# Six thresholds of a list scheduler and two cuts of a chain: when side work joins TensorE's queue in a hybrid diffusion step

## The chip, the cores and the metric

One core of a Trainium2 chip runs the whole program. The metric is device time in microseconds (us), the median over the runs; lower is better. Engines: TensorE (PE) multiplies, VectorE (DVE), ScalarE (ACT) and GpSimd (POOL) do elementwise work, SyncE (SP) issues the transfers from memory.

## The reference

One inference step of a two-layer backbone over 512 latent and 128 context tokens, width 1024. Cut to what matters:

```python
for l in range(2):
    mod = split(silu(c) @ w_mod[l] + b_mod[l], 6)          # once for latents, once for context
    h = rms_norm(x) * (1 + mod[1]) + mod[0]
    if l == 0:                                             # attention next to Hyena
        p = h @ w_in                                       # q, k, v and three Hyena channels
        q, k = rms_norm(q), rms_norm(k)                    # per head of 128, then rotary
        y = softmax(q k') v ;  z = long_conv(v1 * x1, filters) * x0      # by Fourier transforms
        out = concat(y, z) @ w_out
    else:                                                  # mLSTM, 8 heads, forward and backward scans
        out = (norm(fwd(h) + bwd(h)) * sigmoid(o)) @ w_out
    x = x + mod[2] * rms_norm(out)
    h = rms_norm(x) * (1 + mod[4]) + mod[3]
    x = x + mod[5] * rms_norm((gelu(conv3(h @ wu_g)) * conv3(h @ wu_u)) @ w_down)
```

## The kernel before

All 640 tokens stay on the chip; weights stream through once, in tiles of 128x1024, by SP's queue (tile `wr`). Every large product is computed as three products of a high and a low part, so each weight tile is split first: ACT casts the high part (`wh`), DVE subtracts it from the raw tile to get the low part (`wl`). The activations are split likewise (`a0h`/`a0l` into layer 0's mixer, `a1` into its FFN, `a2` and `a3` in layer 1). `wl155` is the low part of tile 155.

The order of the instructions on each engine is decided while the program is built, by a hand-made list scheduler (class `Order`). A main list of tasks is TensorE's: weight column after weight column. Beside it run side generators: the attention's units, the Hyena's filters and long convolution, the mLSTM's directions, the modulation sections, the norms at the boundaries. Each side yields at its waits. Before each piece of main work `pump` looks at the sides in their order and steps one whose time, `when`, has come on TensorE's planned clock:

```python
if s[3] and not r:
    return max(s[0], self.t["DVE"] - s[3], self.t["ACT"] - s[3])
t = max(s[0], self.t["DVE"] - s[4], self.t["ACT"] - s[4])
```

`s[0]` is when the side's inputs are planned to be ready. `s[3]` is nonzero for the modulation sections alone (SLACK0 to SLACK4): they go on only while DVE and ACT are planned no further than that many ns ahead of TensorE. `s[4]` is the same for all other sides (their lead: HLEAD for Hyena, QLEAD for q, k, v, BLEAD for the boundaries, DLEAD for the mLSTM's directions). If no side can step, `pump` lets the next weight tiles be split (`idle`), until DVE or ACT are planned SPARE ns ahead, or TIGHT ns while a boundary is under way. These numbers do no work; they decide in which order the instructions of the engines stand, and each engine then takes its own in that order.

Products accumulate in PSUM: three buffers of kind `mm` (1024 columns or 640 tokens) and two of kind `aux`, handed on when the reading engine has emptied them; a new product waits for a free one.

What the text speaks of:

- A modulation section (`mod_section`, layer l, section s) multiplies silu(c) into 1024 columns of `w_mod`: DVE multiplies and adds transferred weight tiles `mw` into two accumulators `acc` (latents and context). Sections 2 and 5 then split `acc` (ACT `moda`, DVE `modb`), sum over partitions on TensorE with a matrix of ones (`modp`, four matmuls with `moda`, four with `modb`), and DVE adds the result to the row. `acc12` is layer 1, section 2: the gate behind the mLSTM's output projection.
- `direction`: one head and direction of the mLSTM. TensorE: `mb`, `dl`, `it`, `pi`, `in`, `pc`, small matmuls; DVE between them: the weights `w`, the states `cb` and the sums `nu`, `hs`. `hT` transposes the finished head, `mos` gates it, `o1h`/`o1l` are its parts for the output projection `o`. The projections of the next heads (`mq`, `mk`, `mv`, `mo`) are TensorE's main work around them.
- `forward`/`long_conv`: Hyena. DVE multiplies spectra in a chain of ten instructions per frequency block (`vx`, `vf`, then `vp`, `vm`), before the inverse transform on TensorE (`iy`). `u` are the Hyena's projections, `zh` their convolution, `hyf` the products of its filters.
- `qkv_evac`: for each of five token tiles, q and k are copied (`qsq`), normalised (`qn`), scaled, multiplied with the gain (`qkg`) and rotated (`rope`), and then transposed (`qkt`).
- `fm_first`: the first three weight columns of a projection run side by side over the eight blocks of 128 inputs, the last TAILK blocks column by column.
- `o1` is the boundary behind the mLSTM's output projection: the residual, its norm, transposes (`o1p3nt`), shift and scale (`o1p3ny`), the split (`a3h`, `a3l`), then the up-projection (`g10l`, `u10l`: the last 256 tokens of its first columns).

L284 is the line of the helper that records all operations of DVE, ACT, POOL and SP, L365 the matmuls, L376 the transposes: rows are told apart by their tiles.

Of the kernel before, what the change touches and what calls it, by code (L numbers as in the profile page):

```python
# [59 lines left out]
class Order:  # L60
# [7 lines left out]
    LEAD = 3000.0  # L68
    SPARE = 5000.0
    GUARD = 0.0  # L70
    TIGHT = 2000.0
    FIRST = 2500.0

    def __init__(self):
# [116 lines left out]
    def pump(self):  # L191
        while True:
# [7 lines left out]
            else:  # L200
                spare = self.TIGHT if self.urgent else self.SPARE
                if self.urgent:
# [123 lines left out]
def hybrid_step(ctx: ExitStack, tc: tile.TileContext, A: dict, O: dict):  # L326
# [27 lines left out]
    def mm(name):  # L354
        t = mmp.tile([P, 1024], F32, tag="mm", name=name)
        od.got("mm", t)
        return t
# [39 lines left out]
    def rsqrt(ss, n, scale, name, eps=EPS, v=None):  # L397
        y, q, a = (small(name + c, n) for c in "yqa")
        if v is None:
            v = small(name + "v", n)  # L400
            nc.vector.tensor_scalar(v, ss, scale, eps, op0=ALU.mult, op1=ALU.add)
        nc.vector.tensor_scalar(y.bitcast(I32), v.bitcast(I32), -0.5, RSQ, op0=ALU.mult, op1=ALU.add)
        nc.vector.scalar_tensor_tensor(q, v, -0.5, y, op0=ALU.mult, op1=ALU.mult)
        for n in range(3):
            nc.vector.tensor_tensor(a, q, y, op=ALU.mult)
            if n < 2:
                nc.vector.scalar_tensor_tensor(q, a, 1.5, q, op0=ALU.add, op1=ALU.mult)
            nc.vector.scalar_tensor_tensor(y, a, 1.5, y, op0=ALU.add, op1=ALU.mult)
        return y
# [17 lines left out]
                yield  # L427

    EVF = 1
    TAILK = 3  # L430

    def fm_task(src, act, name, evac, needs=()):
        def run(w):
# [89 lines left out]
    def fm_first(specs, act):  # L523
# [9 lines left out]
        def all_(_):  # L533
            ps = []
            for n in range(3):
                od.take("mm")
                ps.append(mm(specs[n][1]))
            seq = [(k, n) for k in range(KT - TAILK) for n in range(3)]
            seq += [(k, n) for n in range(3) for k in range(KT - TAILK, KT)]
            for k, n in seq:  # L540
# [368 lines left out]
    HYE = nc.vector  # L909
    ROPE = nc.gpsimd  # L910
    SLACK1 = 1500.0
    SLACK2 = 2000.0
    SLACK3 = 500.0
    SLACK4 = 500.0

    def spawn_mods(slack, *sections, keys=()):
        def run(_):
            od.spawn(mod_chain(sections, keys), low=slack, rank=MRANK)
            yield
        return Task(run)  # L920
# [105 lines left out]
    def boundary(pss, tiles, l, s, xs, nxt, name, key, pages=None):  # L1026

        n = len(tiles)
        ss = small(name + "ss", n)
        t = {}  # L1030
        yield [("mod", l, s)] + [("mod", 1, 4)] * (l == 0 and s == 5)
        junk = page(name + "j").bitcast(BF)[:, 0:D]
        if WARM and tiles[0] == 0 and nxt is not None:
            nc.scalar.activation(ones1, ones[:, 0:1], AF.Gelu if s == 2 else AF.Exp)
        for j, i in enumerate(tiles):
            if nxt is not None and i >= ROWS:
                t[i] = mw.tile([P, D], F32, tag="mw", name=f"{name}t{i}")
            else:
                t[i] = row(f"{name}t{i}")
            nc.scalar.activation(junk, pss[i], AF.Square, accum_out=ss[:, j : j + 1])  # L1040
            nc.vector.tensor_tensor(t[i], pss[i], mods[l, s, 0 if i < 4 else 1], op=ALU.mult)
            od.gave("mm", pss[i])
            yield 0
        od.side_after(ss)
        yield
        r = rsqrt(ss, n, 1.0 / D, name)
        for j, i in enumerate(tiles):
            nc.vector.scalar_tensor_tensor(xs[i], t[i], r[:, j : j + 1], xs[i], op0=ALU.mult, op1=ALU.add)
            yield 0
            if nxt is None:  # L1050
                nc.sync.dma_start(O["y"][i * P : (i + 1) * P, :], xs[i])
        if nxt is None:
            return
        yield from pre_norm(xs, tiles, l + (s == 5), 3 if s == 2 else 0, nxt, name + "n", key, t, pages)
# [57 lines left out]
    def forward(src, cols, out, name):  # L1112
# [24 lines left out]
        for n, (o, x, y, op) in enumerate(((out[0][:, a], c[:, a], c[:, b], ALU.add), (out[0][:, b], c[:, a], c[:, b], ALU.subtract),  # L1137
# [5 lines left out]
            nc.vector.tensor_tensor(o, x, y, op=op)  # L1143
            if FINE and n % FINE == FINE - 1:
                yield 0
        yield

    FINE = 0

    def filters():  # L1150
        z, w = hy["z"], hy["w"]
# [160 lines left out]
    def long_conv(hf):  # L1312
# [17 lines left out]
        HYE.tensor_tensor(vp[:, h1], vp[:, h1], gr, op=ALU.mult)  # L1330
        if FINE:
            yield 0
# [8 lines left out]
        for n in range(2):  # L1341
# [4 lines left out]
            HYE.tensor_tensor(S, S, gc, op=ALU.mult)  # L1346
            if FINE:
                yield 0
            nc.vector.tensor_tensor(x[0], x[0], x[1], op=ALU.subtract)
            nc.vector.tensor_tensor(C, C, S, op=ALU.add)  # L1350
            if FINE:
                yield 0
# [41 lines left out]

    QROWS = 2
    QACT = 1
    QSCALE = 1

    def qkv_evac(ps, i):
        yield [("qk", j) for j in range(i - QROWS)]  # L1400
# [18 lines left out]
        r = rsqrt(ss, 6, 1.0 / DH, f"qn{i}")  # L1419
        if QSCALE:  # L1420
            for a in range(6):
# [116 lines left out]
    def out_proj(mix, wname, order, l, nxt, xs, halves, name):  # L1538
# [9 lines left out]
        for t in tm_tasks(  # L1548
                lambda k, i, g: [x[:, i * P : (i + 1) * P] for x in cur[k]],
                lambda k: A[wname][order[k] * P : (order[k] + 1) * P, :], KT, halves, name,  # L1550
                lambda ps, t: od.spawn(boundary(ps, t, l, 2, xs, nxt, f"{name}p{t[0]}", "af", name),
                                       lead=BLEAD, urgent=True),
                prep=prep, needs=lambda k, g: [key(q) for q in range(KT)], stay=STAY[l], whole=True,
# [39 lines left out]
    def ffn(l, act, nxt, xs):  # L1593
        hid, cur = {}, {}
        specs = up_specs(l, act, hid)
        ka, kb = (("af", l, h[0]) for h in HALVES)
        ts = fm_head(specs[:NPRE], act, ka, kb)
        ts += [fm_task(s, act, n, f) for s, n, f in specs[NPRE:]]

        def prep(k, g):  # L1600
            c0, c1 = HALVES[g][0] * P, HALVES[g][-1] * P + P
            hh, hl = page(f"hh{l}{k}{g}", FR), page(f"hl{l}{k}{g}", FR)
            split(hh[:, 0 : c1 - c0], hl[:, 0 : c1 - c0], hid[k][:, c0:c1])
            cur[g, k] = hh, hl

        for t in tm_tasks(
                lambda k, i, g: [x[:, (i - HALVES[g][0]) * P : (i - HALVES[g][0]) * P + P] for x in cur[g, k]],
                lambda k: A["w_down"][l, k * P : (k + 1) * P, :], NJ, HALVES, f"dn{l}",
                lambda ps, t: od.spawn(
                    finish_last(ps, t, l, xs) if l == 1 and t == HALVES[1]  # L1610
                    else boundary(ps, t, l, 5, xs, nxt, f"f{l}p{t[0]}", "am"), lead=FLEAD, urgent=True),
                prep=prep, tail=l == 1):
            ts += t
        return ts
# [251 lines left out]
    def head_mix(h):  # L1866
# [30 lines left out]
        for d in range(2):  # L1897
            od.spawn(direction(h, d, q, v1, kw[d], ssb, cb[d], hs, co), lead=DLEAD)
        yield [("hs", h)]
# [56 lines left out]
    J1 = 1  # L1956
    QLEAD = 6000.0
    ALEAD = 6000.0
    BLEAD = 4000.0
    FLEAD = 1000.0  # L1960
    MLEAD = 2500.0
    TLEAD = 1500.0
    DLEAD = 1750.0
    OLEAD = 5000.0
    ms = [x for i in range(4) for x in (4 + i, 8 + i)]
    k0, k1 = act_keys("am", 0, HALVES[0]), act_keys("am", 0, HALVES[1])
# [35 lines left out]
    act2 = Lazy("a2")  # L2002
    tasks.append(spawn_mods(SLACK2, (1, 0), (1, 1), (0, 5), (1, 3), (1, 4), keys=[("hid", 0, J0)]))
    tasks += ffn(0, act1, act2, xs)
# [299 lines left out]
```

## Time and profile before

| what | value |
|---|---|
| median of 3 runs | 1741.65 us (1736.06 to 1744.64) |
| the profiled execution's own time | 1739.15 us |
| its span in the profile | 1737.3 us |
| PE busy | 1683.4 us, 97% of the span |
| DVE, ACT, POOL busy | 1243.6, 746.3, 353.8 us |
| transfers | 203.85 MB, 117 GB/s on average |

A matmul shows as busy from its start to its modelled end, and neighbours overlap, so the busy time tells where TensorE stood still and not how fast it went. How fast is told by the granted clock (PEclk): 1.00 is 2.4 GHz, 0.50 is 1.2 GHz, and a stretch of 20 us at 0.66 is one in which some of the time was at the lower of the two.

### The profile page before, as it was taken

The numbers are of one execution on the slowest core, as the hardware profiler recorded it, in microseconds if no ns is written. First come the engines' busy times: TensorE is split into PE (matmuls) and PEld (weight loads), VectorE is DVE, ScalarE is ACT, GpSimd is POOL, SyncE is SP. The second block draws the span as 40 slices with busy tenths as digits, with TensorE's granted clock in tenths as the row PEclk, the third lists the DMA queues.
The fourth block names the chain that finished last, engine by engine and source line by source line (L and its number), as shares of the span: only waits on it lengthen the run. The fifth ranks groups of instructions, "written<-read, shape, count | busy, mean of one in ns | idle before, by whom it ended". The sixth has DMA issues, their size and how long they took to land. (4 is left out here: it accounts for less than half of the span.)

```text
span 1737.3 us, 25489 instructions
## 1 busy us (share of the span) xinstructions
PE 1683.4 (97%) x10074; PEld 1523.0 (88%) x10074; DVE 1243.6 (72%) x2057; ACT 746.3 (43%) x1233; POOL 353.8 (20%) x187
## 2 busy tenths in 40 slices
PE   7899899999999999999999999997999999999997
PEld 2778787789999999888899999996899999998886
DVE  4788797878878888797766888886578744445365
ACT  3422545545434344455565344334354423333343
POOL 0000121001546454340013111120015411111000
PEclk9999999999999999999999999998999999999999
DMA  9245132412434434454523212122124322223343
GB/s 359 91 152 170 37 101 101 169 38 99 158 121 143 144 119 154 153 198 129 188 89 137 70 47 83 57 69 100 49 77 147 125 77 74 73 74 109 132 159 122
DMA packets 64352, 203.85 MB, mean 117 GB/s; under 512 B 7335, under 2 KB 12455, under 8 KB 64234
## 3 DMA queue, kind: packets, MB, share of 16 engines
q1 hardware_dynamic: 64234, 202.23, 33.9%
q8 instruction: 79, 1.29, 0.3%
q14 instruction: 39, 0.32, 0.1%
HBM read 196.17 MB, written 3.94 MB: 115 GB/s over the span
## 5 line engine op out<-in xcount | busy, mean ns | idle before, releaser
L284 DVE TENSOR_TENSOR wl<-wr,wh 128x1024 fp32r<-128x1024 f32 (+1 forms) x260 | 317.9, 1228 | 107.8 <-ACT wh L284 107.6
L284 ACT CAST wh<-wr 128x1024 fp32r<-128x1024 f32 (+1 forms) x260 | 263.5, 1018 | 146.7 <-PE dn L365 104.1
L284 POOL TENSOR_TENSOR hid<-zg,zu 128x640 f32<-128x640 f32 x44 | 105.5, 2398 | 318.5 <-DVE zu L284 305.9
L284 DVE SCALAR_TENSOR_TENSOR acc<-mw,sc,acc 128x1024 f32<-128x1024 f32 x91 | 168.3, 1868 | 2.7 <-DMA mw<-in_w_mod 2.4
L284 POOL TENSOR_TENSOR acc<-acc,modp 128x1024 f32<-128x1024 f32 x49 | 146.2, 2984 | 115.4 <-ACT modp L284 91.2
L284 DVE SCALAR_TENSOR_TENSOR zg<-g,vec,zg 128x127 f32<-128x127 f32 (+3 forms) x168 | 87.4, 541 | 89.4 <-ACT zg L284 86.4
L365 PE MATMUL dn<-wh,hh 128*128 128x512 f32 x440 | 139.1, 396 | 1.8 <-DVE zu L284 1.6
L365 PE MATMUL dn<-wl,hh 128*128 128x512 f32 x440 | 138.2, 394 | 0.0
L365 PE MATMUL dn<-wh,hl 128*128 128x512 f32 x440 | 138.1, 394 | 0.0
L284 DVE SCALAR_TENSOR_TENSOR zu<-u,vec,zu 128x511 f32<-128x511 f32 (+2 forms) x164 | 86.7, 549 | 62.8 <-ACT zu L284 59.9
L284 ACT ACTIVATE zu<-u,vec 128x640 f32<-128x640 f32 (+1 forms) x42 | 36.8, 876 | 173.8 <-PE u L365 173.8
L365 PE MATMUL u<-a3h,wh 128*128 128x384 f32 (+1 forms) x336 | 104.7, 312 | 0.8 <-DVE a3h L284 0.8
L365 PE MATMUL g<-a3h,wh 128*128 128x384 f32 (+1 forms) x336 | 104.8, 312 | 0.0
L365 PE MATMUL g<-a1h,wh 128*128 128x384 f32 (+1 forms) x336 | 104.8, 312 | 0.0
L365 PE MATMUL u<-a3l,wh 128*128 128x384 f32 (+1 forms) x336 | 104.1, 310 | 0.5 <-POOL a3l L284 0.5
L365 PE MATMUL u<-a3h,wl 128*128 128x384 f32 (+1 forms) x336 | 104.3, 310 | 0.2 <-DVE wl L284 0.2
L365 PE MATMUL u<-a1h,wl 128*128 128x384 f32 (+1 forms) x336 | 104.2, 310 | 0.2 <-DVE wl L284 0.2
L365 PE MATMUL u<-a1h,wh 128*128 128x384 f32 (+1 forms) x336 | 104.2, 310 | 0.0
L365 PE MATMUL g<-a3h,wl 128*128 128x384 f32 (+1 forms) x336 | 104.1, 310 | 0.0
L365 PE MATMUL g<-a3l,wh 128*128 128x384 f32 (+1 forms) x336 | 104.1, 310 | 0.0
L365 PE MATMUL g<-a1h,wl 128*128 128x384 f32 (+1 forms) x336 | 104.0, 310 | 0.0
L365 PE MATMUL u<-a1l,wh 128*128 128x384 f32 (+1 forms) x336 | 104.0, 310 | 0.0
(742 smaller groups left out, 4452.2 us busy)
## 6 DMA issues: line engine op xcount, KB each, us to landing
wr<-in_w_up SPq DMA_DIRECT2D x92, 512.0 KB, 3.3
wr<-in_w_down SPq DMA_DIRECT2D x82, 512.0 KB, 3.3
mw<-in_w_mod SPq DMA_DIRECT2D x80, 512.0 KB, 4.4
wr<-in_w_ml SPq DMA_DIRECT2D x34, 512.0 KB, 3.6
wr<-in_w_out SPq DMA_DIRECT2D x18, 512.0 KB, 4.2
wr<-in_w_in SPq DMA_DIRECT2D x13, 512.0 KB
wr<-in_w_u SPq DMA_DIRECT2D x12, 512.0 KB, 5.2
we<-in_w_mod SPq DMA_DIRECT2D x8, 512.0 KB, 7.3
```

Source lines behind the costliest of these rows:

```text
L284: r = f(*args, **kw)
L365: r = nc.tensor.matmul(out, lhsT, rhs, start=start, stop=stop)
```

## The change

The weights, the transfers and the products stay the same; TensorE's generated order has 8181 rows in both. Six numbers move thresholds or leads of the scheduler. FINE lets the Hyena's DVE chain yield after every second product, so that other instructions can be put between. QSCALE moves the scaling of q and k from ACT (six multiplies of 128x128 per token tile) to DVE (one multiply of 128x768 with the factor broadcast), five token tiles in all.

```diff
--- before.py
+++ after.py
@@ -68,7 +68,7 @@
     LEAD = 3000.0
     SPARE = 5000.0
     GUARD = 0.0
-    TIGHT = 2000.0
+    TIGHT = 6000.0
     FIRST = 2500.0
 
     def __init__(self):
@@ -427,7 +427,7 @@
                 yield
 
     EVF = 1
-    TAILK = 3
+    TAILK = 2
 
     def fm_task(src, act, name, evac, needs=()):
         def run(w):
@@ -909,7 +909,7 @@
     HYE = nc.vector
     ROPE = nc.gpsimd
     SLACK1 = 1500.0
-    SLACK2 = 2000.0
+    SLACK2 = 4000.0
     SLACK3 = 500.0
     SLACK4 = 500.0
 
@@ -1145,7 +1145,7 @@
                 yield 0
         yield
 
-    FINE = 0
+    FINE = 2
 
     def filters():
         z, w = hy["z"], hy["w"]
@@ -1394,7 +1394,7 @@
 
     QROWS = 2
     QACT = 1
-    QSCALE = 1
+    QSCALE = 0
 
     def qkv_evac(ps, i):
         yield [("qk", j) for j in range(i - QROWS)]
@@ -1956,11 +1956,11 @@
     J1 = 1
     QLEAD = 6000.0
     ALEAD = 6000.0
-    BLEAD = 4000.0
+    BLEAD = 6000.0
     FLEAD = 1000.0
     MLEAD = 2500.0
     TLEAD = 1500.0
-    DLEAD = 1750.0
+    DLEAD = 4000.0
     OLEAD = 5000.0
     ms = [x for i in range(4) for x in (4 + i, 8 + i)]
     k0, k1 = act_keys("am", 0, HALVES[0]), act_keys("am", 0, HALVES[1])
```

The generated order, at three places.

TensorE at the start of the mLSTM's output projection, where head 7's last main work `mo7` ends and the first tiles `o10_0`, `o10_1` begin. Before:

```order
L365 MATMUL mo7_11153<-a2l7_7690,wh154_10884 128x256
L365 MATMUL in71_11233<-v17_9003,w71_10986 128x129 x4
L365 MATMUL pc71_11254<-kw71_10839,v17_9003 128x128
L365 MATMUL pc71_11254<-v17_9003,kw71_10839 128x1
L365 MATMUL modp1200_11282<-moda120_11262,onesr_91 128x512
L365 MATMUL modp1200_11282<-modb120_11263,onesr_91 128x512
L376 MATMUL hT7_11286<-ident_86,hs7_10917 128x128 x5
L365 MATMUL modp1201_11303<-moda120_11262,onesr_91 128x512
L365 MATMUL modp1201_11303<-modb120_11263,onesr_91 128x512
L365 MATMUL o10_0_11311<-wh155_11016,o1h0_11020 128x512 x2
L365 MATMUL o10_0_11311<-wh155_11016,o1l0_11021 128x512 x2
```

The same place now:

```order
L365 MATMUL mo7_11197<-a2l7_7665,wh154_10952 128x256
L376 MATMUL hT7_11277<-ident_86,hs7_10899 128x128 x5
L365 MATMUL o10_0_11284<-wh155_11076,o1h0_11080 128x512 x2
L365 MATMUL o10_0_11284<-wh155_11076,o1l0_11081 128x512 x2
L365 MATMUL o10_0_11284<-wl155_11077,o1h0_11080 128x512 x2
L365 MATMUL o10_1_11301<-wh155_11076,o1h0_11080 128x512 x2
L365 MATMUL o10_1_11301<-wh155_11076,o1l0_11081 128x512 x2
L365 MATMUL o10_1_11301<-wl155_11077,o1h0_11080 128x512 x2
```

The last scan's `in71` and `pc71` and the partition sums `modp` of section (1,2) are gone from here (the sums stand among `mk5` and `mo2`, the scan among `mo5` and `mo6`); the transposes `hT7` follow `mo7`, and the projection follows them.

DVE when head 4's two directions begin. Before:

```order
L284 TENSOR_TENSOR kw40_9932<-kT4_9926,col_8329 128x640
L284 TENSOR_TENSOR kw41_9934<-kT4_9926,col_8329 128x640
L284 SCALAR_TENSOR_TENSOR acc120_8352<-mw126_8992,sc_93,acc120_8352 128x1024
L284 SCALAR_TENSOR_TENSOR w40_9966<-mb40_9963,col_8329,msk_7719 128x128 x5
L284 SCALAR_TENSOR_TENSOR zmq5_9986<-mq5_9897,vec_84,zmq5_9986 128x511 x2
L284 SCALAR_TENSOR_TENSOR zmq5_9986<-mq5_9897,vec_84,zmq5_9986 128x127 x2
L284 TENSOR_TENSOR wl146_9993<-wr146_9683,wh146_9992 128x1024
L284 SCALAR_TENSOR_TENSOR cb40_9922<-cb40_9922,wsb_8387,dl40_10023 128x129 x3
L284 SCALAR_TENSOR_TENSOR zmq5_9986<-tmq5_10030,zmq5_9986 128x640
L284 SCALAR_TENSOR_TENSOR w41_10048<-mb41_10045,col_8329,msk_7719 128x128 x5
L284 SCALAR_TENSOR_TENSOR zmk5_10068<-mk5_9998,vec_84,zmk5_10068 128x511 x2
```

The same place now:

```order
L284 TENSOR_TENSOR kw40_9903<-kT4_9897,col_8304 128x640
L284 TENSOR_TENSOR kw41_9905<-kT4_9897,col_8304 128x640
L284 TENSOR_TENSOR modb120_9932<-acc120_8327,moda120_9931 128x1024
L284 SCALAR_TENSOR_TENSOR w40_9938<-mb40_9935,col_8304,msk_7694 128x128 x5
L284 SCALAR_TENSOR_TENSOR cb40_9893<-cb40_9893,wsb_8362,dl40_9946 128x129 x3
L284 SCALAR_TENSOR_TENSOR w41_9956<-mb41_9953,col_8304,msk_7694 128x128 x5
L284 SCALAR_TENSOR_TENSOR cb41_9894<-cb41_9894,wsb_8362,dl41_9976 128x129 x3
L284 SCALAR_TENSOR_TENSOR zmq5_9995<-mq5_9880,vec_84,zmq5_9995 128x511 x2
L284 SCALAR_TENSOR_TENSOR zmq5_9995<-mq5_9880,vec_84,zmq5_9995 128x127 x2
L284 TENSOR_TENSOR wl146_10002<-wr146_9673,wh146_10001 128x1024
L284 TENSOR_TENSOR nu40_10020<-it40_10021,col_8304 128x516
L284 TENSOR_TENSOR acc120_8327<-modp1200_10036,modn12_9929 128x512
```

The second direction (`w41`, `cb41`) comes right behind the first, ahead of the next head's convolution `zmq5` and the split `wl146`, and the modulation section's `modb120` and its first sum stand here; `modb120` stood some 150 rows later before.

DVE in layer 0, in the second half of q, k, v and Hyena, where the split `wl24` for the last Hyena projections stands. Before:

```order
L284 TENSOR_TENSOR vf13_1598<-vf13_1598,g1c_953 128x512
L284 TENSOR_TENSOR vx01_1873<-vx01_1873,vx11_1874 128x512
L284 TENSOR_TENSOR vf12_1597<-vf12_1597,vf13_1598 128x512
L284 TENSOR_TENSOR vp11_1971<-vx01_1873 128x256
L284 TENSOR_TENSOR vp11_1971<-vf12_1597 128x256
L284 TENSOR_TENSOR vm11_1972<-vx01_1873 128x256
L284 TENSOR_TENSOR vm11_1972<-vf12_1597 128x256
L284 SCALAR_TENSOR_TENSOR zh1_2001<-u1_1919,vec_84,zh1_2001 128x511 x2
L284 SCALAR_TENSOR_TENSOR zh1_2001<-u1_1919,vec_84,zh1_2001 128x127 x2
L284 TENSOR_TENSOR wl24_2015<-wr24_1757,wh24_2014 128x1024
L284 TENSOR_TENSOR qsq3_1779<-qsq3_1779,rope_1119 128x6x64 x2
```

The same place now:

```order
L284 TENSOR_TENSOR qsq4_1799<-qsq4_1799,qn4y_1922 128x768
L284 TENSOR_TENSOR qsq3_1780<-qsq3_1780,qkg_1121 128x768
L284 TENSOR_TENSOR vx01_1758<-vf12_1611,g1c_953 128x512
L284 TENSOR_TENSOR vx11_1759<-vf13_1612,g1s_972 128x512
L284 TENSOR_TENSOR vf12_1611<-vf12_1611,g1s_972 128x512
L284 TENSOR_TENSOR vf13_1612<-vf13_1612,g1c_953 128x512
L284 SCALAR_TENSOR_TENSOR zh1_1989<-u1_1914,vec_84,zh1_1989 128x511 x2
L284 SCALAR_TENSOR_TENSOR zh1_1989<-u1_1914,vec_84,zh1_1989 128x127 x2
L284 TENSOR_TENSOR wl24_2003<-wr24_1741,wh24_2002 128x1024
L284 TENSOR_TENSOR qsq3_1780<-qsq3_1780,rope_1119 128x6x64 x2
L284 SCALAR_TENSOR_TENSOR zh2_2052<-u2_1995,vec_84,zh2_2052 128x511 x2
L284 SCALAR_TENSOR_TENSOR zh2_2052<-u2_1995,vec_84,zh2_2052 128x127 x2
```

Six instructions of the chain (the two sums, `vp11`, `vm11`) went behind `wl24`; the scaling of `qsq4` on DVE, and ahead of it its eleven small instructions `qn4`, went in front.

## Rows read from the trace of the kernel before

**Rows 1.** Page: busy share in 40 slices of the span, and granted clock.

```profile
PE   7899899999999999999999999997999999999997
...
PEclk9999999999999999999999999998999999999999
```

**Rows 2.** Waits of TensorE: for what, us in total, times, longest.

```profile
PE modp L365 <- ACT moda L284: 6.3, 1, 6.3
PE qkv L365 <- DVE wl L284: 4.4, 1, 4.4
PE u L365 <- DVE wl L284: 3.5, 3, 3.1
```

**Rows 3.** Windows: length, busy by engine (instructions), PEclk, DMA share, GB/s.

```profile
180.00:200.00 20.00, 15.56 (x80) 12.98 (x79) 13.56 (x41) 8.82 (x35) 1.96 (x2) 0.91 0.19 53
240.00:260.00 20.00, 16.85 (x104) 16.59 (x103) 19.56 (x36) 4.60 (x13) 7.39 (x4) 0.91 0.08 27
...
405.00:880.00 475.00, 473.58 (x2869) 441.99 (x2869) 378.09 (x461) 223.81 (x288) 178.43 (x70) 1.00 0.43 147
947.00:1180.00 233.00, 232.45 (x1718) 230.82 (x1717) 193.06 (x472) 96.88 (x199) 40.75 (x29) 1.00 0.21 68
1180.00:1200.00 20.00, 11.28 (x54) 9.16 (x53) 16.45 (x37) 8.64 (x20) 1.49 (x1) 0.66 0.44 155
1260.00:1300.00 40.00, 37.57 (x253) 35.98 (x253) 30.97 (x75) 22.82 (x40) 6.36 (x6) 1.00 0.23 75
```

**Rows 4.** Timeline of TensorE, start of the output projection.

```profile
1190.01 0.79 PE L365 MATMUL modp<-moda,onesr 128*128 128x512 f32 x1 [6.25 <-ACT moda L284]
1191.27 0.79 PE L365 MATMUL modp<-modb,onesr 128*128 128x512 f32 x1 [0.47 <-DVE modb L284]
1194.06 1.30 PE L376 MATMUL hT<-ident,hs 128*128 128x128 f32 x5 [2.00 <-DVE hs L284]
...
1198.57 1.05 PE L365 MATMUL o<-wh,o1h 128*128 128x512 f32 x2
...
1199.95 0.63 PE L365 MATMUL o<-wl,o1h 128*128 128x512 f32 x2
1200.42 0.39 PE L365 MATMUL modp<-moda,onesr 128*128 128x512 f32 x1
```

**Rows 5.** Timeline of DVE, layer 0, second half.

```profile
230.88 2.36 DVE L284 TENSOR_TENSOR wl<-wr,wh 128x1024 fp32r<-128x1024 f32 x2 [1.14 <-ACT wh L284]
...
242.90 2.06 DVE L284 TENSOR_TENSOR vx<-vf,g1c 128x512 f32<-128x512 f32 x1
...
248.33 0.68 DVE L284 TENSOR_TENSOR vx<-vx,vx 128x512 f32<-128x512 f32 x1
...
250.87 2.16 DVE L284 SCALAR_TENSOR_TENSOR zh<-u,vec,zh 128x511 f32<-128x511 f32 x4
252.95 1.22 DVE L284 TENSOR_TENSOR wl<-wr,wh 128x1024 fp32r<-128x1024 f32 x1
...
258.46 0.16 DVE L284 TENSOR_SCALAR qn4v<-qss 128x6 f32<-128x6 f32 x1
...
260.21 0.17 DVE L284 SCALAR_TENSOR_TENSOR qn4y<-qn4a,qn4y 128x6 f32<-128x6 f32 x1
```

**Rows 6.** Timeline of POOL, same place.

```profile
242.25 2.16 POOL L284 TENSOR_TENSOR vx<-zh,vx 128x640 f32<-128x640 f32 x1 [19.29 <-ACT qj L284]
```

**Rows 7.** Timeline of TensorE, same place.

```profile
254.22 0.69 PE L365 MATMUL u<-a0h,wl 128*128 128x384 f32 x1 [3.15 <-DVE wl L284]
```

**Rows 8.** Tile qsq: operation, count, ns min/median/max, first and last start.

```profile
L284 ACT ACTIVATE qsq<-qsq,qn4y x6: 384/386/403, 260.4 to 261.9; 128x128 f32<-128x128 f32 x6
...
L284 DVE TENSOR_TENSOR qsq<-qsq,qkg x5: 948/949/953, 194.7 to 263.6; 128x768 f32<-128x768 f32 x5
```

**Rows 9.** Timeline of all engines, mLSTM, head 1.

```profile
984.72 1.12 DVE L284 SCALAR_TENSOR_TENSOR cb<-cb,wsb,dl 128x129 f32<-128x129 f32 x3 [0.40 <-PE dl L365]
...
986.27 1.06 PE L365 MATMUL it<-cb,zmq 128*128 128x129 f32 x8
```

## The prediction

> **What bounds the kernel now.** I read the page first: TensorE is busy in nearly every slice, and the dips are few and sharp [rows 1]. So time can be won only where TensorE stands still or runs at the lower clock, and lost only where a new wait appears. The table of its waits says which ones end last: one of 6.3 us for a modulation section's cast, 4.4 us for a weight split in the first half of layer 0, 3.1 us of the 3.5 for the split in its second half [rows 2]. The windows say how much the rest can give: the FFN of layer 0 has 473.58 us of 475 busy, the mLSTM 232.45 of 233, both at clock 1.00; the start of the output projection has only 11.28 of 20, at 0.66 [rows 3]. Transfers and the total of DVE's work end no such wait, so I go by places and not by engine totals. All sums are against the profiled execution (1739.15 us); the median lies 2.5 us above it.
>
> **Start of the output projection.** Before, TensorE reaches the section's sums with nothing else to do: 6.25 us for `moda`, 0.47 for `modb`, 2.00 for `hs`, together 8.72 us [rows 4]. The wait comes from the order: the cast stands behind the last head's work on ACT and DVE, and the transposes of the last head and all of the projection stand behind the sums on TensorE. Behind the idle time the clock fell: the window's 0.66 of 20 us says 6.8 us lost, so 13.6 us at 1.2 GHz [rows 3]. The `modp` at 1190.01 lasts 0.79 us and that at 1200.42 0.39, and the pairs of `o` fall from 1.05 to 0.63 between 1198.57 and 1199.95 [rows 4], so the low stretch is 1186.0 to 1199.6. In it TensorE idled 4.0 + 0.47 + 2.00 us and worked 7.1, of which half, 3.55, is lost. The place costs 8.72 + 3.55 = 12.3 us.
>
> In the new order the sums stand a whole head earlier, the last scan's `in71` and `pc71` too, so `hs7` is long done when `mo7` ends; `hT7` and then `o10_0` follow without a wait. The eight `modp` are moved and cost the same at full clock. What may come instead: the third token tile needs the PSUM buffer that `hT7` leaves, which `mos7` on DVE frees, and `mos7` now stands behind four tiles' splits. I put 0.3 us there, with bounds of 0 and 2.0 (the size of the wait for `hs` that it replaces). **-12.0 us** (-12.3 to -10.3).
>
> **What that puts into the mLSTM.** DVE takes over two `modb`, each a 128x1024 subtract like `wl` at 1.22 us, and four sums of 128x512 at some 0.68 like `vx` [rows 5]: 5.2 us. DVE works 193.06 of 233 us there [rows 3], so 40 us are free and the work fits; the cover is gone only where a direction is due. DLEAD lets DVE take up a direction while it is further ahead in its plan, and puts both directions back to back. In the trace of before, `cb` of head 1 ended at 985.84 and `it` began at 986.27: a margin of 0.43 us and no wait [rows 9]. After the change most of the 16 directions should run at such margins. A small matmul that waits holds up all main work behind it on TensorE. If every second direction waits for a tenth of a us it is 0.8; if all wait 0.25, 4.0. I take the nearest row, which is no wait at 0.43 of margin, and add a little: **+0.5** (0 to +4).
>
> **Layer 0, second half.** The split `wl24` came 3.15 us late [rows 7], and the window's 0.91 of 20 us means 3.6 us at 1.2 GHz [rows 3], nearly all of it busy behind the wait: 1.7 lost. FINE takes six instructions of the chain away from in front of it, 248.33 to 250.87, 2.5 us [rows 5]. But the order also puts two scalings in front, which cost 0.95 each by the gain multiply of the same shape [rows 8], and the eleven instructions `qn4`, 258.46 to 260.38 or 1.9 us [rows 5]: 3.8 us. Against that, the six products of the first chain move ahead of `wl22`, where DVE waited 1.14 us for ACT [rows 5]; and the multiplies beside POOL's work took 2.06 us instead of 0.68 at worst [rows 5, 6], which may fall otherwise. So the wait becomes 3.15 - 2.5 + 3.8 - 1.14 = 3.3 if the multiplies are as slow as before, and about 0.5 if they are not (some 2.8 us less over the four). I take 1.5, and that the clock then stays up (if not, 1.7 come back): -1.65 - 1.7 = -3.3. The transposes of the last tiles and the inverse transform now come before scores that waited little before; I give 1.3 us back. ACT is spared 5 x 6 multiplies of 0.386 us and reading gaps [rows 8], but nothing waits for ACT for long there. **-2** (-4 to +2).
>
> A rule speaks against this part. The multiply `vx` that began at 242.90 beside POOL's operation of 2.16 us ended with it [rows 5, 6]. The Trainium skill, "SBUF — State Buffer", section "Who interferes with whom", says that a VectorE instruction with two SBUF inputs and a GpSimd instruction that reads SBUF exclude each other for a whole instruction; this trace agrees at 242.90. QSCALE's new multiplies are of that kind, while ACT's were not; by the rule the sum would be that of the second rival.
>
> **First half of layer 0.** The 4.4 us for a split [rows 2] and the 0.91 behind it [rows 3] stay: there DVE's rows are in the same order as before, FINE's yields notwithstanding. **0.**
>
> **Boundary o1.** 40 us lose 2.4 [rows 3], all in waits for the last normalised blocks. TIGHT and BLEAD put three weight splits ahead of the norm's small chain, where DVE idled, and the transposes of the last two token tiles about nine matmuls earlier; TAILK moves the last blocks' use. I take **-1.5** (-2.4 to +1).
>
> **FFN of layer 0.** SLACK2 lets the modulation's multiply-adds go ahead of some splits; 97 us of DVE are free in 475 [rows 3], TensorE loses 1.4 in all, so nothing to win. **0** (0 to +2). The filters' products in layer 0 change places with projections: **-0.5** (-2 to +1.5). FFN of layer 1 and the end have the same order.
>
> Sum: -12.0 + 0.5 - 2 + 0 - 1.5 + 0 - 0.5 = -15.5, so 1723.65 against 1739.15, and 1741.65 - 15.5 = 1726 for the median.
>
> **Rivals.**
> 1. *The directions eat half.* Speaking for it: margins of 0.43 us where there were often several, and DVE with 5 us more. Against: no wait in the two heads that already ran this way. At 0.4 us over 16 directions, 6.4 instead of 0.5: 1732.
> 2. *POOL and the scalings collide.* The two scalings ahead of `wl24` each last as long as POOL's operation, 2.16 instead of 0.95, and push two products into the same: up to 4 us more in front of `wl24`, so the wait is 5.5 and the low clock (1.7) stays: +5.7, 1732. For it, 242.90; against, POOL's operations there follow the gain multiply, not the scaling.
> 3. *The wait moves and stays.* The projection's next need, `mos7` and the high and low parts of the last heads' outputs, comes so late that TensorE waits over 5 us and the clock falls again: 1726 + 5 + 3.5 = 1735. Against: DVE has 3 us between the end of `mo7` and the third tile for one 0.9 us operation.
> 4. *Slower.* A direction taken up early on DVE holds the splits `wl` and the convolutions of the next head behind it: in-order DVE serves two directions at a stretch, some 8 us with `nu` and `hs`. If a main projection then waits for its `wl` once per head by more than 3 us, as at `wl24`, and the clock falls behind it as there, each head costs 3 + 1.7 = 4.7, eight heads 37.6 against 16 won: 1764. It decides from 3.0 us per head on (24.2 over eight heads takes all of 15.5 and 8.7 beyond). Against: in the mLSTM window TensorE lost 0.55 us in 233 at a DVE load of 83%, so the splits run well ahead.
>
> **Numbers.** The forecast 0.62, rival 1 0.14, rival 2 0.06, rival 3 0.08, slower 0.07, faster than all this (the 4.4 us go too) 0.03. Faster and slower count from 0.5%, 8.7 us, about what a measurement of this kernel can tell from no change: the limit is 1733. The forecast, the last case and half of rivals 1 and 2 lie below it, with some of the forecast's own spread taken off: faster 0.74, same 0.18, slower 0.08. The forecast's bounds are -12.3 - 4 - 2.4 - 2 = -20.7 and -10.3 + 4 + 2 + 1 + 2 + 1.5 = +0.2, hardly all at once; its own range is 1720 to 1732, and the range up to rival 3, 1718 to 1738.
>
> **What would show it.** Right: no wait for `moda` between the mLSTM and the projection, and clock 1.00 in that window; TensorE over 19 us busy there. The mLSTM's window still loses under 2 us. The wait before the last Hyena projections shrinks to 0 to 3 us; that for `qkv` at the first half's end stays at 4.4. The boundary loses about 1 us in 40. Wrong: waits of several tenths at `it`, `pi` or `dl`; a wait of over 2 us at the third token tile; a lower clock anywhere in layer 1.

## The result and the profile after

The changed kernel takes 1727.5 us (median of 5 runs, 1723.8 to 1729.08) against 1740.36 (5 runs, 1736.06 to 1744.64): ratio 0.9924, 95% interval 0.9901 to 0.9947. The profiled execution took 1723.8 us, span 1722.0.

The page of the changed kernel, busy share and granted clock in 40 slices, to lay beside [rows 1]: the dip at three quarters of the line (slice 28) is gone from both.

```profile
PE   7899999999999999999999999999999999999997
...
PEclk9999999999999999999999999999999999999999
```

TensorE's waits after, beside [rows 2] (for what, us in total, times, longest). The 6.3 us for `moda` are no longer there. The longest wait for `zu` grew from 1.0 to 3.0 us, and one of 0.8 for `mos` is new (its row is below); the two splits of layer 0 are still late.

```profile
PE u L365 <- DVE wl L284: 3.8, 2, 3.6
PE dn L365 <- DVE zu L284: 3.5, 2, 3.0
...
PE qkv L365 <- DVE wl L284: 3.0, 1, 3.0
```

The windows after, beside [rows 3] (length, busy time of PE, PEld, DVE, ACT, POOL, PEclk, DMA share, GB/s). The start of the output projection went from 11.28 us of 20 busy at 0.66 to 19.23 at 1.00, the boundary from 37.57 of 40 to 39.94. The FFN of layer 0 went the other way, 473.58 to 471.27, and the second half of layer 0 is no better (0.91 to 0.83).

```profile
180.00:200.00 20.00, 16.97 (x95) 14.30 (x94) 16.14 (x44) 9.54 (x39) 1.99 (x2) 1.00 0.13 40
240.00:260.00 20.00, 16.37 (x92) 16.08 (x91) 19.62 (x35) 3.31 (x6) 6.21 (x4) 0.83 0.18 59
405.00:880.00 475.00, 471.27 (x2842) 439.17 (x2841) 371.17 (x454) 221.54 (x281) 174.17 (x69) 1.00 0.43 147
947.00:1180.00 233.00, 232.41 (x1715) 229.64 (x1714) 200.95 (x496) 97.39 (x206) 41.18 (x29) 1.00 0.21 69
1180.00:1200.00 20.00, 19.23 (x100) 16.18 (x100) 14.17 (x18) 11.88 (x18) 1.42 (x1) 1.00 0.55 184
1260.00:1300.00 40.00, 39.94 (x287) 39.28 (x286) 28.61 (x61) 22.15 (x37) 10.51 (x8) 1.00 0.33 109
```

TensorE's timeline at the start of the projection, beside [rows 4]. `hT` has no wait, `o` runs at 0.62 to 0.74 us per pair, and the one gap is at the third token tile, 0.77 us for `mos7`.

```profile
1184.76 0.71 PE L376 MATMUL hT<-ident,hs 128*128 128x128 f32 x5
1185.23 0.70 PE L365 MATMUL o<-wh,o1h 128*128 128x512 f32 x2
...
1189.07 0.74 PE L365 MATMUL o<-wh,o1h 128*128 128x512 f32 x2 [0.77 <-DVE mos L284]
```

Where the time went is read best by stretches. The generated order tells which matmul of the trace is the first of which column, so the same columns can be found in each trace; the table takes the start of each against its start in the trace before, and the difference between two of them is what a stretch won or lost. The columns: `o00_0` opens layer 0's output projection, `u021` is the last up-projection of its FFN, `gates` opens the mLSTM, `vT5` is a transpose early in it, `o11_3` is in the mLSTM's output projection, `g12l` follows the boundary o1, `dn11_3` is near the end.

| stretch (us won: minus) | after | the same kernel again | SLACK2 back | DLEAD and TIGHT alone | DLEAD alone | all but DLEAD |
|---|---|---|---|---|---|---|
| start to `o00_0` | -2.69 | -2.47 | -2.38 | -1.63 | -2.31 | -3.52 |
| to `u021` | +0.51 | +2.04 | +0.72 | +0.63 | +5.58 | +1.70 |
| to `gates` (FFN, layer 0) | +4.05 | +4.22 | +1.09 | +1.04 | -0.02 | +5.46 |
| to `vT5` | -2.94 | 0.00 | -2.91 | -2.94 | -2.94 | -0.02 |
| to `o11_3` (mLSTM, projection) | -11.15 | -11.15 | -10.73 | -11.15 | -10.68 | -0.01 |
| to `g12l` (boundary o1) | -3.23 | -3.24 | -2.95 | -3.25 | +0.05 | -3.32 |
| to `dn11_3` | +0.14 | +0.10 | -0.53 | -0.15 | +0.25 | -1.31 |
| sum | -15.31 | -10.50 | -17.69 | -17.45 | -10.07 | -1.02 |

The columns of one kernel in two executions ("after" and "again") show what belongs to the order: the mLSTM with its projection, the boundary and the FFN agree within 0.2 us; two stretches in between differ by 1.5 and 2.9 and belong to the execution. Two executions are few, though. Two further traces with the same order in the FFN ("all but DLEAD" and "the scan early, the section late" below) have +5.46 and +4.23 us there, and four with SLACK2 at 2000 and TIGHT at 6000, again of one order, have 1.03 to 1.09 three times and once, with DLEAD 6000, 2.82. So the FFN varies by one or two us as well.

### The profile page after: what moved, and what is told of

Read it like the earlier page. It is cut to its first block, busy times and chain, and to the rows that moved or that the text cites. A ratio compares the mean times of both kernels' runs of the same rounds, so it can differ in the third digit from the quotient of the medians.

```text
span 1722.0 us, 25452 instructions
## 1 busy us (share of the span) xinstructions
PE 1678.4 (97%) x10074; PEld 1519.7 (88%) x10074; DVE 1245.8 (72%) x2062; ACT 737.7 (43%) x1203; POOL 349.9 (20%) x187
## 5 line engine op out<-in xcount | busy, mean ns | idle before, releaser
L284 DVE TENSOR_TENSOR wl<-wr,wh 128x1024 fp32r<-128x1024 f32 (+1 forms) x260 | 323.0, 1248 | 112.2 <-ACT wh L284 112.0
L284 POOL TENSOR_TENSOR acc<-acc,modp 128x1024 f32<-128x1024 f32 x49 | 141.6, 2890 | 115.4 <-ACT modp L284 115.1
L365 PE MATMUL g<-a1l,wh 128*128 128x384 f32 (+1 forms) x336 | 104.2, 310 | 0.0
```

Source lines behind the costliest of these rows:

```text
L284: r = f(*args, **kw)
L365: r = nc.tensor.matmul(out, lhsT, rhs, start=start, stop=stop)
```

## The experiments

All ratios are against runs of the kernel before on the same chip. The diff changes seven numbers: five thresholds or leads (TIGHT, TAILK, SLACK2, BLEAD, DLEAD; the title and the text on the change count six), FINE and QSCALE. My theory before the first four: the wait in front of the output projection went because DLEAD moved two things out of that place, the section's sums and the last scan; the rest nearly cancels. The rival: the section alone was the cause (theory A below; theory B is that both count), or the other numbers share in the gain.

**DLEAD alone.**

```diff
-    DLEAD = 1750.0
+    DLEAD = 4000.0
```

> The kernel before with DLEAD at 4000 and nothing else changed. My theory: the gain at the start of the output projection (11.5 us by the two profiles) comes from DLEAD alone, and the rest of the change nets to little: 1740.4 - 11.5 = 1729, ratio 0.993, no wait for moda in front of the projection. Rival: the section and the last scan need the other numbers too (TIGHT, SLACK2); then the waits of 6.3 and 2.0 us stay and the ratio is 0.998 or more.

1729.85 us, ratio 0.9954 (0.9934 to 0.9974): the expected time, and no wait for `moda` in front of the projection. The window of the projection's start is as in the full change:

```profile
1180.00:1200.00 20.00, 19.45 (x103) 16.54 (x102) 15.25 (x19) 13.66 (x20) 1.89 (x2) 1.00 0.55 162
```

The place won 10.68 us. The 5.58 lost on the way to `u021` are in rows whose order is that of before: in the boundary of layer 0's output projection DVE waited 4.89 us for the transfer of a modulation tile (`mw`), so `moda` came 2.9 us late, and the clock of that window was 0.91. In the kernel before DVE waited 1.6 us there.

```profile
346.45 4.87 DVE L284 SCALAR_TENSOR_TENSOR acc<-mw,sc,acc 128x1024 f32<-128x1024 f32 x4 [4.89 <-DMA mw<-in_w_mod]
...
351.26 0.49 PE L365 MATMUL modp<-moda,onesr 128*128 128x512 f32 x1 [2.90 <-ACT moda L284]
```

**The change without DLEAD** (DLEAD 1750, all else as changed).

> The changed kernel with DLEAD back at 1750. My theory: the 11.5 us at the start of the output projection come back and the boundary o1 (3 us), the first half of layer 0 (3) and the FFN of layer 0 (minus 4) nearly cancel: 1727.5 + 11.5 = 1739, ratio 0.999 to the kernel before. Rival: the clock stretches and the boundary are the gain: ratio 0.996 or less.

1737.38 us, ratio 0.9982 (0.9964 to 1.0). The waits of before are back, those for `zu` stay; the boundary's 3.3 us are won too. Theory and number agree: the other six together are worth about 3 us by the runs, with anything from nothing to 6 us inside the interval.

```profile
PE modp L365 <- ACT moda L284: 6.6, 2, 6.3
...
PE dn L365 <- DVE zu L284: 3.5, 2, 3.0
...
PE hT L376 <- DVE hs L284: 2.0, 1, 2.0
```

**The section early, the scan late.**

```diff
-    SLACK3 = 500.0
+    SLACK3 = 1000.0
```

> The kernel before with SLACK3 at 1000 instead of 500: the sums of section (1,2) move to head 2's projections, but the last scan (in71) still follows mo7 and the transposes hT7 still stand ahead of the projection. Theory A (the section's cast is the cause): the place is free, 1740.4 - 12 = 1728, ratio 0.993. Theory B (two late things stand in front of the projection, and either alone holds it): TensorE waits some 7 to 8 us for hs at hT7 in place of 8.7, and the clock falls as before; ratio 0.998 to 1.000, 1737 to 1740.

1743.32 us, ratio 1.0026 (1.0014 to 1.0037). TensorE's waits:

```profile
PE hT L376 <- DVE hs L284: 7.9, 1, 7.9
...
PE kT L376 <- DVE zmk L284: 5.5, 2, 3.7
```

Theory A falls: with the sums 200 us earlier (at 985 us instead of 1190) TensorE waits 7.9 us at the same place for `hs`, because `in71` and the norm of the last head stand where they stood. Theory B has its wait, but its 1737 to 1740 us are missed by 3: the 5.5 us for `zmk`, the price of the section's multiply-adds in front of the convolutions, weren't in it.

**The scan early, the section late** (the change with SLACK3 lower).

```diff
-    SLACK3 = 500.0
+    SLACK3 = -500.0
```

> The changed kernel with SLACK3 at -500: the directions run early as in the change, but the sums of section (1,2) come late, now among the projection's second tile, behind about 50 of its matmuls. Theory A: TensorE waits for moda again, 5 us or more, ratio 0.996 or more. Theory B: the scan was the part that had to be early; the section's cast has time beside the projection, so the place costs under 2 us: ratio 0.992 to 0.993, 1727 to 1729.

1737.14 us, ratio 0.9992 (0.9975 to 1.0009). Both expectations were wrong: the ratio is theory A's, but not by its wait (1.2 us for `moda` at the most). The place itself is free (19.23 of 20 at 1.00), as theory B said, but the time did not follow: the section's row is needed again some 40 us later, for the gate at the boundary o1. DVE adds its last sum at 1227.74 and the first gated tile follows at 1228.35; TensorE waits 2.0 us at `o1p0t` and 2.7 at `a3h`, with the boundary's window at 37.11 of 40 and clock 0.91. In the full change that section is long done and DVE starts the first gated tile at 1212.79. By columns, the stretch to `o11_3` won only 7.35 us, and the one to `g12l` lost 4.13 where the full change won 3.23. So the section has to be early as well, for a later reader. TensorE's longest waits, the two windows, and DVE's rows at the end of the section (line `acc<-modp,modn`):

```profile
PE u L365 <- DVE a3h L284: 2.7, 1, 2.7
...
PE o L365 <- DVE o1p0t L284: 2.0, 1, 2.0
```

```profile
1180.00:1200.00 20.00, 19.23 (x119) 17.32 (x118) 17.24 (x32) 12.38 (x18) 3.07 (x3) 1.00 0.54 167
1260.00:1300.00 40.00, 37.11 (x238) 35.72 (x237) 26.02 (x68) 20.19 (x36) 6.45 (x7) 0.91 0.16 53
```

```profile
1227.74 0.69 DVE L284 TENSOR_TENSOR acc<-modp,modn 128x512 f32<-128x512 f32 x1 [1.14 <-PE modp L365]
1228.35 3.48 DVE L284 TENSOR_TENSOR o1p0t<-o,acc 128x1024 f32<-128x1024 f32 x3
```

**Both early by another number** (SLACK3 1500, DLEAD as before).

> The kernel before with SLACK3 at 1500, DLEAD untouched: by the order both the section's sums (among mv7) and the last scan (among mo6) come early. Theory B (both must be out of the way, by whatever number): no wait over 1 us between mo7 and the projection, 11 us won there. But SLACK3 also puts the section's multiply-adds in front of kT's convolution, which cost 5.5 us of waits and some at the lower clock at SLACK3 1000: 8 lost in the mLSTM, so 1737, ratio 0.998. Rival (only DLEAD frees the place): waits of 6 us or more remain at hT or modp.

1746.56 us, ratio 1.0041 (1.0025 to 1.0056). Both numbers were wrong. The place is not free: `hT` waits 5.31 us. DVE's rows tell why: the scan is done, but the norm of the last head (`hn7`, from 1200.09 until its last product `hs` ends at 1203.41) stands behind the splits `wl` and `o1l` of the projection; its inputs were there at 1192.1. In the full change `hn7` stands ahead of those splits, at 1174.07. Theory B as I wrote it was too coarse: the whole chain of the last head has to stand in front of the splits on DVE, not only the scan's matmuls on TensorE. No run freed the place by another number than DLEAD, so the rival isn't refuted as far as the number goes.

```profile
1198.15 1.29 DVE L284 TENSOR_TENSOR wl<-wr,wh 128x512 fp32r<-128x512 f32 x2
1199.35 0.82 DVE L284 TENSOR_TENSOR o1l<-mos,o1h 128x640 fp32r<-128x640 f32 x1
1200.09 0.71 DVE L284 TENSOR_SCALAR hn7v<-hss 128x5 f32<-128x5 f32 x1
...
1202.59 0.82 DVE L284 TENSOR_TENSOR hs<-hs,hn7y 128x640 f32<-128x640 f32 x1
```

```profile
1203.56 1.30 PE L376 MATMUL hT<-ident,hs 128*128 128x128 f32 x5 [5.31 <-DVE ntile L284]
```

**SLACK2 back** (the change with SLACK2 2000).

> The changed kernel with SLACK2 back at 2000. In the profile after, TensorE waits 2.98 us at the first down-projection of layer 0's FFN for zu (1.03 before), with the lower clock behind it, and 0.55 more at hl. Theory A: SLACK2 put one more multiply-add of a modulation section (1.2 us) ahead of that zu on DVE; without it the wait is 1.0 to 1.8, the clock stays up, the FFN loses 1 us instead of 4: 1725, ratio 0.991. Rival B: DVE is simply full there and TensorE came 2 us earlier to it; the wait stays at about 3 us and the time at 1727.5.

1726.89 us, ratio 0.9916 (0.989 to 0.9941). The wait is as before, 1.0 of 1.5 us, the FFN loses 1.09 instead of 4.05, no window of it is below clock 1.00: theory A. By runs the two kernels can't be told apart (1727.5 and 1726.89).

```profile
PE dn L365 <- DVE zu L284: 1.5, 2, 1.0
```

**DLEAD and TIGHT alone.**

> The kernel before with DLEAD 4000 and TIGHT 6000 only. Theory: these two carry the whole gain, 11 us at the start of the projection and 3 at the boundary o1, and the FFN's new wait is not there: 1740 - 14 = 1726, ratio 0.992. Rival: FINE, QSCALE, SLACK2 and TAILK add to the gain; then it is 1730 or more, ratio 0.995.

1722.71 us, ratio 0.9906 (0.9882 to 0.993), the fastest of all, and with the intervals it may be level with the change. The rival's 0.995 lies outside the interval. By the traces it is the change without the FFN's 3 us:

```profile
1180.00:1200.00 20.00, 19.39 (x98) 15.88 (x97) 12.36 (x16) 10.06 (x15) 1.27 (x1) 1.00 0.59 185
1260.00:1300.00 40.00, 39.91 (x290) 39.33 (x288) 29.73 (x59) 22.17 (x35) 12.35 (x9) 1.00 0.32 106
```

**Scaling and chain back** (the change with QSCALE 1 and FINE 0).

> The changed kernel with QSCALE 1 and FINE 0. What the two traces say: the wait before the last Hyena projections is 3.6 us with the change and 3.2 without, the region up to the output projection of layer 0 takes the same time: 1727.5 within 1.5 us, ratio 0.992 to 0.993. By my prediction (2 us won there) it would be 1729.5.

1729.9 us, ratio 0.9936 (0.9914 to 0.9958). The runs don't decide: the median lies 0.9 us outside my range and on the 1729.5 of the prediction, and the interval holds both. Up to `o00_0` the trace won 2.88 us where the change won 2.69 and 2.47, so a gain of 2 us isn't there. What is slower in this profile came later, in stretches that the two don't touch (2.6 us for `moda` at layer 0's boundary, as in the first experiment).

**DLEAD 3000 and 6000, each with TIGHT 6000.**

> The kernel before with DLEAD 3000 and TIGHT 6000. By the generated order the section's sums and the last scan still stand behind mo7, as at 1750. Theory: what counts is whether both have left that place, not how far DVE runs ahead; so the waits of 6 and 2 us are back, TIGHT's 3 us remain: 1737, ratio 0.998. Rival (more lead helps by degrees): half of the way to the kernel with 4000, 1731, ratio 0.994.

1736.58 us, ratio 0.9977 (0.996 to 0.9995): by steps and not by degrees. The waits are back, `moda` 5.5 at the longest and `hs` 2.0.

```profile
PE modp L365 <- ACT moda L284: 7.2, 2, 5.5
...
PE hT L376 <- DVE hs L284: 2.0, 1, 2.0
```

> The same with DLEAD 6000: by the order the sums and the scan stand as at 4000, and the directions are pulled forward still more (191 of TensorE's rows change place). Theory: the mLSTM has margin for it, TensorE waits under 1.5 us in it, and the time is that at 4000, 1722 to 1726, ratio 0.991 to 0.992. Rival (my first and fourth: directions taken early make TensorE wait at it, pi and dl): 3 us or more of such waits, 1727 or more.

1727.24 us, ratio 0.9921 (0.9902 to 0.9939): the rival's number, though the intervals of 4000 and 6000 overlap. The waits lie between the two expectations, 2.5 us in all, and not where I named them: 1.3 us at `mk` for the cast `wh` of a weight tile, 0.8 at `mb` for ACT's `ss`, none at `it`, `dl` or `pi`. By columns the stretch with mLSTM and projection wins 7.93 us instead of 11.15.

```profile
PE mk L365 <- ACT wh L284: 1.3, 1, 1.3
...
PE mb L365 <- ACT ss L284: 0.8, 1, 0.8
```

**The change again**, beside these two.

> The changed kernel itself, beside the other two on one chip. Theory: the FFN's new wait of 3 us and the low clock behind it cost it some 3 us against DLEAD and TIGHT alone: 1727, ratio 0.992, 2 to 4 us above the kernel with DLEAD 6000. Rival: the runs' scatter covers it, and both come out within 1 us.

1728.57 us, ratio 0.9923 (0.9902 to 0.9944), 1.3 us above the kernel with 6000: between the two expectations, and within the scatter of the runs, while the FFN's wait of 3.0 us and its loss of 4.22 are in the trace again.

## Why the prediction came out as it did

The forecast was 1726 and the time is 1727.5. Its largest term was right and for its reason; three smaller ones were wrong and partly made up for each other. That the two times lie only 1.5 us apart is in part luck: the gain was 12.9 us and not 15.5, and 1.3 us of the difference vanish because the median before was 1741.65 in three runs and 1740.36 in five. With the two stretches that vary left out, and 2.0 us of the first row (below), the trace of the change sums to -0.7 + 4.05 - 11.15 - 3.23 = -11.0, against -15.5 forecast; the medians moved by 12.9 and, when the change was run again, by 12.2.

*Start of the output projection and mLSTM*: -12.0 + 0.5 = -11.5 forecast, -11.15 measured in both executions, 10.68 by DLEAD alone. The wait for the third token tile was 0.77 us (0.3 within 0 to 2.0). The mLSTM's window still loses 0.59 us, with no wait over 0.3: rival 1 is refuted at DLEAD 4000. Rival 3's wait was 0.8 instead of 5, rival 4's does not occur. One sign of being wrong, a lower clock in layer 1, is absent from the trace of the change and present in the second one (0.83 at 920 to 940 us), but the kernel before has it there too (0.84). And the sentence that transfers end no wait of TensorE was wrong: the longest of all, 6.4 us before and 6.3 after, is for the tile `hyw` at the program's start; the sum doesn't touch it. What my text lacked is that the section's cast and the last scan were two separate causes, and that the norm behind the scan has a place of its own on DVE; three experiments showed it.

*Layer 0, second half*: -2 forecast, -0.3 to -0.7 measured. The step that failed is the wait before the last projections: 1.5 us taken, 3.63 measured, against 3.15 before. My sum gave 3.3 if the multiplies beside POOL stay as slow as before, and it came to that by another way. The four multiplies took 4.4 us instead of 5.7, but one of the eleven small instructions of `qn4`, put at 0.17 us, took 1.41 beside POOL's operation. Three of DVE's instructions were held so, each of them with two inputs; two ended 0.55 us behind the end of POOL's operation (at 245.77 and 247.19), and `qn4q` together with it. The `vx` of before at 242.90 is of the first kind too: it ended 0.55 us behind POOL's operation, not with it, as the prediction has it.

```profile
239.65 1.41 DVE L284 SCALAR_TENSOR_TENSOR qn4q<-qn4v,qn4y 128x6 f32<-128x6 f32 x1
...
242.45 0.96 DVE L284 TENSOR_TENSOR qsq<-qsq,qn4y 128x768 f32<-128x768 f32 x1
...
244.20 0.69 DVE L284 TENSOR_TENSOR vx<-vf,g1c 128x512 f32<-128x512 f32 x1
244.80 1.52 DVE L284 TENSOR_TENSOR vx<-vf,g1s 128x512 f32<-128x512 f32 x1
246.24 1.50 DVE L284 TENSOR_TENSOR vf<-vf,g1s 128x512 f32<-128x512 f32 x1
```

```profile
239.47 1.57 POOL L284 TENSOR_TENSOR vx<-zh,vx 128x640 f32<-128x640 f32 x1 [21.98 <-issue]
244.43 1.34 POOL L284 TENSOR_TENSOR qrt<-qsq,rope 128x384 f32<-128x384 f32 x1 [3.38 <-DVE qsq L284]
245.73 1.46 POOL L284 TENSOR_TENSOR qru<-qsq,rope 128x384 f32<-128x384 f32 x1
```

The scalings cost what their row of before said, 0.96 us each (0.95), and did not collide with POOL; so rival 2, with the rule behind it, found its neighbours in the chain and in `qn4`, but not the new multiplies. The size comes from all traces: from 194 us to `o00_0`, where the window at 240 to 260 us stands at 0.83, the new order of this part needs 0.4 us less than the old one (four traces against three), and where it stands at 0.91, 0.7 less (one against four; against the trace of before it is 0.3). The window's fall from 0.91 to 0.83 can't be laid to the order from these traces: the old order has both.

*First half of layer 0*: 0 forecast, and the order's effect is 0. The wait there fell to 3.0 us all the same, but it did so in all six traces of experiments with the old order of this part too. What sets the trace of before apart is the clock: there it is low in one longer stretch at 120 to 140 us (0.83), in all the others in two shorter ones, at 120 to 140 and at 160 to 180 (0.91 each). With the later one DVE gets ahead of TensorE before the place, the wait is 1.4 us shorter, and the clock stays at 1.00 behind it (180 to 200) instead of 0.91. That the clock is the cause is argued from the traces; no run set it. I argued from one execution as if it were the kernel. Some 2 us of the first row of the table are this.

*Filters*: -0.5 forecast; -0.8 by the start of `o00_0` in the traces (mean -2.73 of six with TAILK 2, -1.95 of six without). The waits say the same: TensorE's wait for `zh` at `hyf` is 2.3 us in all seven traces with TAILK 3 and 0.4 in all six with TAILK 2, where one of 1.0 for `zh` at `u` comes in its place. Before, and after:

```profile
PE hyf L365 <- DVE zh L284: 2.3, 1, 2.3
```

```profile
PE u L365 <- ACT zh L284: 1.0, 1, 1.0
...
PE hyf L365 <- DVE zh L284: 0.4, 1, 0.4
```

*Boundary o1*: -1.5 forecast (-2.4 to +1), -3.23 measured, and 3.25 by TIGHT where DLEAD is there already. The mechanism was right, the bound too narrow: it counted only the 2.4 us of idle time in the window, all of which went, and 0.8 more came from rows in which TensorE shows as busy; which of them is open. BLEAD had no part: with it back at 4000 the generated order is the same row for row.

*FFN of layer 0*: 0 forecast (0 to +2), +4.05 measured. I looked at DVE's average, 97 us free of 475, and at the splits' margins. The step that failed is that average: at the end of the up-projections DVE was behind, and TensorE came 2 us earlier to a place that DVE sets. SLACK2 put one more multiply-add (88 instead of 87) in front of the last `zu`, whose end frees the PSUM buffer of the third token tile's down-projection. So DVE began that `zu` at 703.13, as late as before (703.30). With SLACK2 back it began at 701.63, while TensorE came to the place only 0.5 us later than in the change. After, and with SLACK2 back:

```profile
703.13 2.16 DVE L284 SCALAR_TENSOR_TENSOR zu<-u,vec,zu 128x511 f32<-128x511 f32 x4
```

```profile
701.63 2.16 DVE L284 SCALAR_TENSOR_TENSOR zu<-u,vec,zu 128x511 f32<-128x511 f32 x4
```

TensorE after:

```profile
705.44 1.19 PE L365 MATMUL dn<-wh,hh 128*128 128x512 f32 x2 [2.98 <-DVE zu L284]
...
707.28 1.06 PE L365 MATMUL dn<-wl,hh 128*128 128x512 f32 x2
...
709.17 0.63 PE L365 MATMUL dn<-wl,hh 128*128 128x512 f32 x2
```

TensorE waited 2.98 us, and the pairs behind it took 1.19 and 1.06 us instead of 0.63 for a while. SLACK2 costs 3 us of the 4; the remaining 1.1 come with TIGHT, at the FFN's last tiles among others (a wait of 0.55 us for `hl`).

## What to carry to other kernels

Where an order is generated, a threshold works by steps: what counts is which instruction stands in front of which at the places where an engine waits, and two late chains at one place must both leave it, each before its own next reader. An engine's average slack says nothing about the place where its queue ends last; look at the stage's end. Before a term of 2 us is read from one profile, see which of its stretches are the same in a second execution of the same kernel.

## What the runs showed of the hardware

The same kernel, profiled twice, differs by 4.8 us of span, and the table says where. The largest part, 2.9 us, lies between `gates` and `vT5` (871 to 927 us in the trace of before): one execution went down to the lower clock there and the other did not, after waits of the same size (0.9 and 0.7 us, and 0.9 and 0.8). Over all kernels the window of 920 to 940 us stands at 1.00 or anywhere down to 0.74. "After", then "the same kernel again":

```profile
920.00:940.00 20.00, 20.00 (x144) 19.52 (x143) 11.78 (x16) 10.43 (x14) 9.18 (x4) 1.00 0.51 178
```

```profile
920.00:940.00 20.00, 19.15 (x116) 18.03 (x116) 9.53 (x16) 8.43 (x14) 4.94 (x3) 0.83 0.39 132
```

And TensorE's clock fell without a wait ahead: between 120 and 140 us it was busy 20.00 of 20 in every trace, at 0.83 in that of before and 0.91 in the others. What stands ahead of the fall in every trace is a run of 32 matmuls of one column each (`modt`, sums of the modulation, 3.6 to 4.0 us). The same run stands ahead of the second fall, at 160 to 180 us; before has it there too, at 166.73, and its clock stayed at 1.00. The window and the run in the trace of before:

```profile
120.00:140.00 20.00, 20.00 (x99) 15.19 (x98) 13.71 (x17) 3.81 (x9) 0.00 (x0) 0.83 0.47 157
```

```profile
121.25 3.98 PE L365 MATMUL modt<-ones,acc 128*128 128x1 f32 x32
```

The second thing that varies is a transfer just in time: at layer 0's boundary the cast `moda` behind the modulation tiles came over 1 us late for TensorE in five of thirteen traces (up to 2.9 us), less than that in two, and on time in six, those of before and after among them. DVE's wait for the `mw` transfer there went from 1.6 us (before) to 5.0. What decides either is open; it wasn't tried.
